# A two-layer diffusion backbone: the second FFN's down projections interleaved with seven-product up steps, and four smaller edits

## The chip, the cores and the metric

One core of one Trainium2 chip. The metric is the device time of one execution in microseconds (us), the median of several runs. The kernel computes in fp32 accuracy: each matrix product is made of three matmuls of operands that were split in a high and a low part.

## The reference

A batch of one, 512 tokens of width 1024, with 256 context tokens. Layer 0 mixes by attention (four global and four windowed heads, rotary positions, a sink), layer 1 by a Fourier transform over tokens and over channel groups, followed by a linear map. Each layer ends with a gated FFN with a width-3 convolution over tokens; every part is normed before and after, and modulated by vectors that come from the condition c.

```python
def conv_ffn(h, w_up, conv_w, conv_b, w_down):
    u = h @ w_up
    up = jnp.pad(u, ((0, 0), (1, 1), (0, 0)))
    u = up[:, :-2] * conv_w[0] + up[:, 1:-1] * conv_w[1] + up[:, 2:] * conv_w[2] + conv_b
    gate, val = jnp.split(u, 2, axis=-1)
    return (jax.nn.silu(gate) * val) @ w_down
...
        if i % 2 == 0:
            y, yc = attention_mixers(h, hc, ...)
        else:
            y = fourier_mix(h) @ w_f
        x = x + g1 * rms_norm(y, norm_g[i, 1])
        h = modulate(rms_norm(x, norm_g[i, 2]), sh2, sc2)
        x = x + g2 * rms_norm(conv_ffn(h, ffn_w_up[i], ...), norm_g[i, 3])
```

The FFN's inner width is 2816, which is 22 chunks of 128.

## The kernel before, in words

Tokens lie along the free dimension: `xT`, `yT`, `hh` and `hl` hold 8 chunks of 128 channels by 512 tokens. `hh` and `hl` are the high and low part of the normed input. `mm3` (lines 97 to 100) makes one product as three matmuls: high by high (L98), low by high (L99) and high by low (L100). `split` (L120, listed as L121) makes the two parts: a cast on ScalarE gives the high part (`wh`, `xh`), a subtraction on VectorE the low part (`wl`, `xl`). In a product the first two matmuls need only the cast of the weights; the third needs the subtraction as well. Weights are loaded by SyncE's queue into three rotating `raw` places and split into five rotating pairs `wh`, `wl`.

An FFN runs 22 up steps, one for each chunk `fi` of the inner width, in three groups `GROUPS` of 8, 6 and 8 chunks. A plain step makes gate and value with 48 matmuls of 512 columns. A seven-product step (`seven_products`, L1138, for the steps in `SEVEN`) computes the same from seven products of half the size in the manner of Strassen, with 84 matmuls of 256 columns; its weights need sums first (`raw` from `raw`, L1124 to L1127), then four splits, here called A (product 1), B (5 and 7), C (6 and 3) and D (2 and 4). ScalarE copies halves of the two results (L1160, L1163), and VectorE adds them (L1166, L1169). After a step the convolution is one ScalarE operation (L1220) and two VectorE taps (L1221, L1223) for each of gate and value, then SiLU, the product of both (L1234), and its split.

After the steps of a group, its down projections follow: for each of the 8 output chunks `d`, one load and split of `w_down`, 3 matmuls of 512 columns for each inner chunk of the group, and a copy (first group) or an add on VectorE (L1341) into `yT`. In the second FFN `pump` advances a modulation product (gemv) between those of group 0: a weight tile `mod_r` is multiplied by a scalar column and added into `gacc` on VectorE (L422, L425).

The order of instructions on each engine is laid out when the program is built, by the order in which the code asks for them and by what each waits for; `follow` adds an order between two instructions. Each engine then takes its instructions in that order.

Other places that the change touches: the attention's projections in groups kb, vb, qa (L841 on), with a gemv (`gemv_early`) pumped between; the first statistic at the start (Squares of `xT` on ScalarE, L652, and a table load, L604); the Fourier weights (`fourier_weights`, L1485 on); the last update of `xT` and the output (L1576 to L1581).

## Time and profile before

| | us |
|---|---|
| median of 3 runs | 1147.99 (1147.73 to 1148.07) |
| the profiled execution | 1147.63 |
| its span | 1145.9 |
| TensorE busy | 1115.4 |
| VectorE busy | 872.4 |
| ScalarE busy | 577.6 |
| GpSimd busy | 176.6 |

The granted TensorE clock of the profiled execution was 0.993. A row of the profile names engine (PE is TensorE, PEld its weight loads, DVE VectorE, ACT ScalarE, POOL GpSimd, SP SyncE), line, operation, and the tiles written and read. In groups the columns are the count, the busy time and the mean in nanoseconds, then idle time ahead of the group and what ended it. Rows of a timeline begin with the start and the duration in us; an operation may start before the one ahead of it has drained, so the pace of a row of operations is read from start to start.

### The profile page before, as it was taken

What the parts mean: (1) busy time and instruction counts of PE and PEld (TensorE: products, weight loads), DVE (VectorE), ACT (ScalarE), POOL (GpSimd) and SP (SyncE); (2) the same over time, 40 slices, a digit from 0 to 9 for tenths busy, and PEclk for the clock granted to TensorE, in tenths of its full rate; (3) what the DMA queues carried; (4) which work ended last, traced back from release to release, by engine and by line L of the source; (5) the groups of instructions that cost most, each with busy time, mean ns of one, the idle gap of its engine ahead of it and who ended that gap; (6) DMA issues with size and microseconds to landing.
All of it is one profiled execution on the core that took longest, in us unless ns stands there. A gap on an engine that the chain in (4) does not pass through costs nothing.

```text
span 1145.9 us, 19121 instructions
## 1 busy us (share of the span) xinstructions
PE 1115.4 (97%) x7658; PEld 962.8 (84%) x7658; DVE 872.4 (76%) x1418; ACT 577.6 (50%) x1030; POOL 176.6 (15%) x184
## 2 busy tenths in 40 slices
PE   8999999999999999999999999899999999999995
PEld 5689988868898978887898898879887888899895
DVE  4678777765679976987998668878997498679745
ACT  4342356666665633552465445557743355256442
POOL 1136332521420000000000143610000000000023
PEclk9999999999999999999999999999999999999998
DMA  9676101075142355535525301920227123223212
GB/s 366 248 239 215 43 1 38 8 263 208 38 184 111 117 194 207 218 122 209 187 108 183 122 2 37 291 88 28 74 95 270 58 92 111 101 84 111 93 56 74
DMA packets 31745, 151.61 MB, mean 132 GB/s; under 512 B 3236, under 2 KB 7972, under 8 KB 19752
## 3 DMA queue, kind: packets, MB, share of 16 engines
q1 hardware_dynamic: 30504, 146.19, 35.9%
q0 software_dynamic: 1152, 4.19, 1.5%
q8 instruction: 60, 0.98, 0.4%
q14 instruction: 29, 0.24, 0.1%
HBM read 146.18 MB, written 4.19 MB: 131 GB/s over the span
## 4 chain that ended last, share of the span: by engine, by line
PE 84%; DVE 7%; ACT 5%; DMA 2%; issue 1%; POOL 0%; DVEq 0%; SPq 0%; ACTq 0%; POOLq 0%
PE mm L98 24%; PE mm L99 23%; PE mm L100 23%; PE PT L920 1%; ACT wh L121 1%; PE O L98 1%; PE gm L498 1%; PE gm L98 1%; PE O L99 1%; PE gm L100 1%; PE gm L99 1%; PE mm L173 1%; PE O L100 1%; DVE md_t L230 1%; DMA xT<-in_mod_r 1%
## 5 line engine op out<-in xcount | busy, mean ns | idle before, releaser
L121 ACT CAST wh<-raw 128x1024 fp32r<-128x1024 f32 (+2 forms) x189 | 180.4, 966 | 188.8 <-PE mm L99 131.3
L121 DVE TENSOR_TENSOR wl<-raw,wh 128x1024 fp32r<-128x1024 f32 (+3 forms) x179 | 203.4, 1144 | 62.8 <-ACT wh L121 62.5
L98 PE MATMUL mm<-hh,wh 128*128 128x256 f32 (+2 forms) x652 | 220.8, 339 | 1.4 <-ACT yT L895 1.0
L99 PE MATMUL mm<-hl,wh 128*128 128x256 f32 (+2 forms) x652 | 218.4, 335 | 0.0
L100 PE MATMUL mm<-hh,wl 128*128 128x256 f32 (+2 forms) x652 | 218.1, 335 | 0.0
L272 POOL TENSOR_TENSOR gacc<-gacc,sq 128x256 f32<-128x256 f32 (+1 forms) x33 | 28.4, 862 | 714.2 <-ACT sq L270 713.5
L98 PEld LDWEIGHTS mm<-hh,wh 128*128 128x128 f32 x652 | 122.5, 188 | 18.9 <-ACT sq L1160 2.8
L99 PEld LDWEIGHTS mm<-hl,wh 128*128 128x128 f32 x652 | 122.6, 188 | 14.0
L100 PEld LDWEIGHTS mm<-hh,wl 128*128 128x128 f32 x652 | 122.6, 188 | 13.8
L98 PE MATMUL mm<-xh,wh 128*128 128x512 f32 (+1 forms) x368 | 132.0, 359 | 0.0
L99 PE MATMUL mm<-xl,wh 128*128 128x512 f32 (+1 forms) x368 | 130.8, 356 | 0.0
L100 PE MATMUL mm<-xh,wl 128*128 128x512 f32 (+1 forms) x368 | 130.3, 355 | 0.0
L98 PE MATMUL mm<-zh,wh 128*128 128x256 f32 x304 | 86.8, 286 | 0.0
L99 PE MATMUL mm<-zl,wh 128*128 128x256 f32 x304 | 84.6, 278 | 0.0
L100 PE MATMUL mm<-zh,wl 128*128 128x256 f32 x304 | 84.3, 277 | 0.0
L98 PEld LDWEIGHTS mm<-xh,wh 128*128 128x128 f32 x368 | 69.3, 188 | 12.8 <-issue 2.1
L99 PEld LDWEIGHTS mm<-xl,wh 128*128 128x128 f32 x368 | 69.2, 188 | 11.1 <-issue 0.4
L100 PEld LDWEIGHTS mm<-xh,wl 128*128 128x128 f32 x368 | 69.2, 188 | 10.8
L1220 ACT ACTIVATE cv<-mm,cols 128x512 f32<-128x512 f32 x64 | 49.6, 776 | 26.5 <-PE mm L100 23.5
L98 PEld LDWEIGHTS mm<-zh,wh 128*128 128x128 f32 x304 | 57.2, 188 | 3.5 <-ACT sq L1163 2.7
L100 PEld LDWEIGHTS mm<-zh,wl 128*128 128x128 f32 x304 | 57.2, 188 | 0.0
L99 PEld LDWEIGHTS mm<-zl,wh 128*128 128x128 f32 x304 | 57.1, 188 | 0.0
(423 smaller groups left out, 2669.3 us busy)
## 6 DMA issues: line engine op xcount, KB each, us to landing
raw<-in_w_up SPq DMA_DIRECT2D x42, 1024.0 KB, 4.9
xT<-in_mod_r SPq DMA_DIRECT2D x20, 1024.0 KB, 4.9
raw<-in_w_down SPq DMA_DIRECT2D x32, 512.0 KB, 4.2
raw<-in_mod_p SPq DMA_DIRECT2D x8, 1024.0 KB, 5.0
raw<-in_w_in SPq DMA_DIRECT2D x6, 1024.0 KB, 7.9
raw<-in_w_down SPq DMA_DIRECT2D x16, 384.0 KB, 3.1
yT<-in_mod_r SPq DMA_DIRECT2D x10, 512.0 KB, 5.9
raw<-in_w_out SPq DMA_DIRECT2D x4, 1024.0 KB, 4.9
```

The source lines that it names most:

```text
L98: i = PE.matmul(out, lhsT=ah, rhs=bh, start=start, stop=False, skip_group_check=skip)
L99: PE.matmul(out, lhsT=ah, rhs=bl, start=False, stop=False, skip_group_check=skip)
L100: return i, PE.matmul(out, lhsT=al, rhs=bh, start=False, stop=stop, skip_group_check=skip)
L121: i = S.copy(out=h, in_=src), eng.tensor_tensor(out=l, in0=src, in1=f(h), op=ALU.subtract)
L173: PE.matmul(ps[:32, :src.shape[1]], lhsT=ones32, rhs=src, start=True, stop=True)
L230: V.scalar_tensor_tensor(out=t, in0=src, scalar=am, in1=R, op0=ALU.mult, op1=ALU.mult)
L272: G.tensor_tensor(out=self.acc[:, sl], in0=self.acc[:, sl], in1=sq[:, sl], op=ALU.add)
L498: PE.matmul(ps[32 * q:32 * q + 32, :], lhsT=spad[:, k, :], rhs=w[:, q * T:(q + 1) * T], start=k == 0, stop=k == KC - 1)
L920: PE.transpose(out=pt[:, j * P:(j + 1) * P], in_=Ps[j][:, off:off + P], identity=ident)
L1220: S.activation(out=cv, in_=ps, func=AF.Identity, bias=bc, scale=wc[1])
```

## The change

The second FFN gets groups of its own: (0,4), (4,6), (10,6) and (16,6), each first chunk and length. All steps from 8 to 21 are seven-product steps. The down projections of the first three groups no longer stand in a block after their group: `DOWN` says how many of them are issued after each up step (four after steps 8 and 9, then one or two). The second gemv goes with the downs of group 1, one `pump` of two operations after each. `xT` is stored to DRAM while the FFN runs, its place takes some of the gate products, and it is loaded again for the end group. In the attention the order of projections is kb, qa, vb, the scores of the first queries are put into the last, and the gemv's second job has two places. A table for the reciprocal root is loaded at the end group of each FFN by an operation on `once`, and the start has a `follow` between Square and table load. Two Fourier weights are loaded early into `yT`. The last update of `xT` is one VectorE operation of 2 x 256 where VectorE and GpSimd did 256 each.

```diff
@@ -30,3 +30,3 @@
 
-GROUPS = [(0, 8), (8, 6), (14, 8)]
+GROUPS = [[(0, 8), (8, 6), (14, 8)], [(0, 4), (4, 6), (10, 6), (16, 6)]]
 
@@ -36,3 +36,5 @@
 
-SEVEN = [(5, 6, 8, 10, 12, 14, 15, 17, 18, 20), (8, 9, 11, 12, 14, 15, 17, 18, 20)]
+SEVEN = [(5, 6, 8, 10, 12, 14, 15, 17, 18, 20), (8, 9, 10, 11, 12, 13, 14, 15, 16, 17, 18, 19, 20, 21)]
+DOWN = {8: 4, 9: 4, 10: 1, 11: 1, 12: 1, 13: 2, 14: 1, 15: 2, 16: 1, 17: 1, 18: 1, 19: 2, 20: 1, 21: 2}
 NSKEW = [6, 5]
...
@@ -462,3 +465,3 @@
                 (l, v), k = jobs[n // KC], n % KC
-                ws[n] = places[n % len(places)]()
+                ws[n] = places[n % len(places) if n < KC else 3 + n % 2]()
                 SY.dma_start(out=ws[n], in_=a["mod_r"][6 * l + v - 2, k // 2][:, k % 2, :])
@@ -479,3 +482,6 @@
                                        op1=ALU.add)
-            load(n + len(places))
+            if n + len(places) < KC:
+                load(n + len(places))
+            for m in {3: (8,), 4: (9,)}.get(n, (n + 2,) if n >= KC else ()):
+                load(m)
             yield
@@ -603,3 +609,3 @@
             S.activation(out=scol, in_=cols[:, C_C:C_C + 16].rearrange("p (a b) -> p a b", a=2), func=AF.Silu)
-            S.activation(out=nsink, in_=scol[:, 0, 0:4], func=AF.Abs_reciprocal_sqrt)
+            ahead = S.activation(out=nsink, in_=scol[:, 0, 0:4], func=AF.Abs_reciprocal_sqrt)
             V.memset(maskb, 0.0)
@@ -651,3 +657,5 @@
                     else:
-                        S.activation(out=sq[:, :n], in_=src[:, k, :], func=AF.Square)
+                        i = S.activation(out=sq[:, :n], in_=src[:, k, :], func=AF.Square)
+                        if nsq[0] == 1:
+                            follow(i, ahead)
                     stat_add(ps, sq, n, k == 0, k == KC - 1)
...
@@ -840,3 +847,3 @@
             blocks = [(hh, hl, 0, 2), (hh, hl, 2, 4), (ch, cl, 0, 0)]
-            for g, kind in enumerate(["kb", "vb", "qa"]):
+            for g, kind in ((0, "kb"), (2, "qa"), (1, "vb")):
                 ws = group_weights(g)
...
@@ -851,3 +858,3 @@
                         pump(pr, 4)
-                        pump(gate, 2 if kind == "vb" else 1)
+                        pump(gate, 2 if kind == "qa" else 1)
                     if kind == "vb":
@@ -857,7 +864,6 @@
                     else:
-                        if t0 == 0:
-                            keys(0, [(mk(pps, [P, T], F32, "misc", 2), n) for n in (2, 4)])
-                        else:
-                            v_kv.append(values(0))
                         q_out(0, t0, ps)
+                    if kind == "vb" and kb == 2:
+                        keys(0, [(mk(pps, [P, T], F32, "misc", 2), n) for n in (2, 4)])
+                        v_kv.append(values(0))
 
...
@@ -1235,3 +1242,3 @@
             if (fi - f0) % 2 == 0:
-                gs["t"] = xp.pair([P, 2, T])
+                gs["t"] = places.pop(0) if l and (f0 == 0 or f0 == 10 and fi < 14) else xp.pair([P, 2, T])
             gh, gl = (t[:, (fi - f0) % 2, :] for t in gs["t"])
@@ -1240,2 +1247,26 @@
 
+        def down_part(gi, w, g_, d, hs, ps=None, end=False):
+            ps, sl = y_mm(pps, w, g_, hs, True, ps)
+            if gi == 0:
+                S.copy(out=yT[:, d, sl], in_=ps[:, sl])
+            else:
+                V.tensor_tensor(out=yT[:, d, sl], in0=yT[:, d, sl], in1=ps[:, sl], op=ALU.add)
+            if end:
+                ys.add(pps, yT[:, d, sl], hs)
+        def down_weights(gi, nch, d, pairs):
+            r = raw([P, nch, P], a["w_down%d%d" % (l, gi)][d])
+            wh, wl = pairs([P, nch, P])
+            split(wh, wl, r)
+            return [(wh[:, c, :], wl[:, c, :]) for c in range(nch)]
+        def down_tiles(gi, nch, g_):
+            yield
+            for d in range(KC):
+                down_part(gi, down_weights(gi, nch, d, wpair), g_, d, [0, 1])
+                if gi:
+                    pump(gem, GP[1])
+                yield
 
@@ -1297,2 +1328,5 @@
             remod(1, *n2, R[1], eng=V)
+            SY.dma_start(out=away, in_=xT)
+            xp2 = mk(cp, [P, 2, 2, 2, T], F32R, "xT")
+            places = [(xp2[:, i, 0], xp2[:, i, 1]) for i in (0, 1, 0, 1)]
             first[skew] = first[skew][:3] + (mk(pps, [P, T], F32, "mm", 6),)
@@ -1316,4 +1350,5 @@
             :, :, NF:], scalar1=-1.0, scalar2=None, op0=ALU.mult)
-        for gi, (f0, nch) in enumerate(GROUPS):
-            end = gi == len(GROUPS) - 1
+        down = iter(())
+        for gi, (f0, nch) in enumerate(GROUPS[l]):
+            end = gi == len(GROUPS[l]) - 1
             for fi in range(max(f0, FIRST), f0 + nch):
@@ -1332,3 +1367,13 @@
                     pump(gem, GP[0])
+                if l:
+                    pump(down, DOWN.get(fi, 0))
+            pump(down, 100)
+            if l and end:
+                xT = mk(cp, [P, KC, T], F32, "xT")
+                SY.dma_start(out=xT, in_=away)
             g_ = [gs[fi] for fi in range(f0, f0 + nch)]
+            if l and not end:
+                down = down_tiles(gi, nch, g_)
+                pump(down)
+                continue
             ws = {}
@@ -1336,15 +1381,6 @@
             def part(d, hs, ps=None):
-                ps, sl = y_mm(pps, ws[d], g_, hs, True, ps)
-                if gi == 0:
-                    S.copy(out=yT[:, d, sl], in_=ps[:, sl])
-                else:
-                    V.tensor_tensor(out=yT[:, d, sl], in0=yT[:, d, sl], in1=ps[:, sl], op=ALU.add)
-                if end:
-                    ys.add(pps, yT[:, d, sl], hs)
+                down_part(gi, ws[d], g_, d, hs, ps, end)
 
             def weights(d):
-                r = raw([P, nch, P], a["w_down%d" % gi][l, d])
-                wh, wl = (xp.spare if end and 4 <= d < 7 else wpair)([P, nch, P])
-                split(wh, wl, r)
-                ws[d] = [(wh[:, c, :], wl[:, c, :]) for c in range(nch)]
+                ws[d] = down_weights(gi, nch, d, xp.spare if end and 4 <= d < 7 else wpair)
 
@@ -1354,2 +1390,4 @@
             if end:
+                S.activation(out=once, in_=g_[-1][0][:, 0:1].bitcast(F32), func=AF.Abs_reciprocal_sqrt, bias=eps, scale=0.0)
                 pump(gem, 100)
@@ -1484,4 +1522,10 @@
 
+        def fourier_load(d):
+            r = yT[:, 2 * d + 2:2 * d + 4, :].rearrange("p a (g i c) -> p (a g) i c", i=2, c=P)
+            SY.dma_start(out=r, in_=a["w_f"][d])
+            return r
         def fourier_weights(d, eng=G):
-            r = raw([P, 4, 2, P], a["w_f"][d])
+            r = f_first[d] if d < 2 else raw([P, 4, 2, P], a["w_f"][d])
 
@@ -1517,2 +1561,3 @@
         over_channels(2, 1)
+        f_first = [fourier_load(d) for d in range(2)]
         r1 = plain.columns(1, pps)
@@ -1578,4 +1623,3 @@
             V.tensor_tensor(out=t, in0=yT[:, k:k + 2, hb], in1=R.unsqueeze(1).to_broadcast([P, 2, HT]), op=ALU.mult)
-            for i, eng in enumerate((V, G)):
-                eng.tensor_tensor(out=xT[:, k + i, hb], in0=xT[:, k + i, hb], in1=t[:, i, :], op=ALU.add)
+            V.tensor_tensor(out=xT[:, k:k + 2, hb], in0=xT[:, k:k + 2, hb], in1=t, op=ALU.add)
             SY.dma_start(out=a["out"][:, k:k + 2, hb], in_=xT[:, k:k + 2, hb])
...
```

What this does to the order on VectorE. First, two neighbouring seven-product steps. In before this is step 18, second of a pair, whose weight tiles are raw_10783 and raw_10785; the names mm_10620 and cv_15xx belong to step 16's plain work and to step 17 (mm_10677).

```order
1258 L1223 SCALAR_TENSOR_TENSOR cv_1530_10645<-mm_10620,cols_64,cv_1530_10645 128x511
1259 L1127 TENSOR_TENSOR raw_10785<-raw_10785,raw_10783 128x512
1260 L1234 TENSOR_TENSOR cv_1530_10645<-cv_1526_10612,cv_1530_10645 128x512
1261 L121 TENSOR_TENSOR wl_10790<-raw_10783,wh_10789 128x512
1262 L121 TENSOR_TENSOR wl_10794<-raw_10785,wh_10793 128x1024
1263 L121 TENSOR_TENSOR xl_10652<-cv_1530_10645,xh_10651 128x512
1264 L121 TENSOR_TENSOR wl_10798<-raw_10785,wh_10797 128x1024
1265 L1166 TENSOR_TENSOR mm_10677<-mm_10677,sq_10679 128x512
1266 L121 TENSOR_TENSOR wl_10802<-raw_10783,wh_10801 128x1024
1267 L1169 TENSOR_TENSOR mm_10678<-mm_10678,sq_10680 128x512
1268 L1221 SCALAR_TENSOR_TENSOR cv_1547_10771<-mm_10677,cols_64,cv_1547_10771 128x511
1269 L121 TENSOR_TENSOR wl_10916<-raw_10913,wh_10915 128x1024
```

Now step 16 to step 17: mm_10612 and mm_10613 are the results of step 16, mm_10726 is its down, raw_10746 and raw_10748 and the wl tiles 10753, 10757, 10761 and 10765 are splits A to D of step 17.

```order
1268 L1172 TENSOR_TENSOR mm_10612<-mm_10612,sq_10614 128x512
1269 L1132 TENSOR_TENSOR raw_10748<-raw_10748,raw_10746 128x512
1270 L123 TENSOR_TENSOR wl_10753<-raw_10746,wh_10752 128x512
1271 L1228 SCALAR_TENSOR_TENSOR cv_1541_10706<-mm_10612,cols_64,cv_1541_10706 128x511
1272 L1175 TENSOR_TENSOR mm_10613<-mm_10613,sq_10615 128x512
1273 L1230 SCALAR_TENSOR_TENSOR cv_1541_10706<-mm_10612,cols_64,cv_1541_10706 128x511
1274 L1133 TENSOR_TENSOR raw_10748<-raw_10748,raw_10746 128x512
1275 L1228 SCALAR_TENSOR_TENSOR cv_1542_10710<-mm_10613,ncw_8780,cv_1542_10710 128x511
1276 L1253 TENSOR_TENSOR yT_68<-yT_68,mm_10726 128x512
1277 L1230 SCALAR_TENSOR_TENSOR cv_1542_10710<-mm_10613,ncw_8780,cv_1542_10710 128x511
1278 L123 TENSOR_TENSOR wl_10757<-raw_10748,wh_10756 128x1024
1279 L1241 TENSOR_TENSOR cv_1542_10710<-cv_1541_10706,cv_1542_10710 128x512
```

```order
1280 L123 TENSOR_TENSOR wl_10761<-raw_10748,wh_10760 128x1024
1281 L123 TENSOR_TENSOR xl_10717<-cv_1542_10710,xh_10716 128x512
1282 L123 TENSOR_TENSOR wl_10765<-raw_10746,wh_10764 128x1024
1283 L123 TENSOR_TENSOR wl_10877<-raw_10874,wh_10876 128x768
1284 L1130 TENSOR_TENSOR raw_10902<-raw_10900 128x1024
```

Before, the four splits stood ahead of the two PSUM adds and the taps of the step before, with one PSUM add between; now the taps and the add of the down (L1253) of the step before stand ahead of splits B, C and D.

Second, VectorE around the gemv (`gacc`). In before it stands among the downs of group 0, whose splits are wl of 128x1024.

```order
1104 L422 TENSOR_SCALAR gacc_9229<-raw_9230,scol_77 128x1024
1105 L425 SCALAR_TENSOR_TENSOR gacc_9229<-raw_9230,scol_77,gacc_9229 128x1024
1106 L1221 SCALAR_TENSOR_TENSOR cv_1328_9161<-mm_9136,cols_64,cv_1328_9161 128x511
1107 L1223 SCALAR_TENSOR_TENSOR cv_1328_9161<-mm_9136,cols_64,cv_1328_9161 128x511
1108 L425 SCALAR_TENSOR_TENSOR gacc_9229<-raw_9238,scol_77,gacc_9229 128x1024
1109 L1234 TENSOR_TENSOR cv_1328_9161<-cv_1324_9128,cv_1328_9161 128x512
1110 L425 SCALAR_TENSOR_TENSOR gacc_9229<-raw_9238,scol_77,gacc_9229 128x1024
1111 L121 TENSOR_TENSOR xl_9074<-cv_1328_9161,xh_9073 128x512
1112 L121 TENSOR_TENSOR wl_9245<-raw_9242,wh_9244 128x1024
1113 L425 SCALAR_TENSOR_TENSOR gacc_9229<-raw_9274,scol_77,gacc_9229 128x1024 x2
1114 L121 TENSOR_TENSOR wl_9281<-raw_9278,wh_9280 128x1024
```

Now it stands among seven-product steps: here step 11 (mm_9765, mm_9766, with its down mm_9877) and the weights of step 12 (raw_9901, raw_9903, split A is wl_9908).

```order
1171 L428 SCALAR_TENSOR_TENSOR gacc_9738<-raw_9897,scol_78,gacc_9738 128x1024
1172 L1172 TENSOR_TENSOR mm_9765<-mm_9765,sq_9767 128x512
1173 L428 SCALAR_TENSOR_TENSOR gacc_9738<-raw_9897,scol_78,gacc_9738 128x1024
1174 L1175 TENSOR_TENSOR mm_9766<-mm_9766,sq_9768 128x512
1175 L1228 SCALAR_TENSOR_TENSOR cv_1426_9859<-mm_9765,cols_64,cv_1426_9859 128x511
1176 L1130 TENSOR_TENSOR raw_9903<-raw_9901 128x1024
1177 L1230 SCALAR_TENSOR_TENSOR cv_1426_9859<-mm_9765,cols_64,cv_1426_9859 128x511
1178 L1228 SCALAR_TENSOR_TENSOR cv_1427_9863<-mm_9766,ncw_8780,cv_1427_9863 128x511
1179 L1253 TENSOR_TENSOR yT_68<-yT_68,mm_9877 128x512
1180 L1230 SCALAR_TENSOR_TENSOR cv_1427_9863<-mm_9766,ncw_8780,cv_1427_9863 128x511
1181 L1132 TENSOR_TENSOR raw_9903<-raw_9903,raw_9901 128x512
1182 L1241 TENSOR_TENSOR cv_1427_9863<-cv_1426_9859,cv_1427_9863 128x512
```

```order
1183 L1133 TENSOR_TENSOR raw_9903<-raw_9903,raw_9901 128x512
1184 L123 TENSOR_TENSOR wl_9908<-raw_9901,wh_9907 128x512
1185 L123 TENSOR_TENSOR xT_8669<-cv_1427_9863,xT_8669 128x512
1186 L123 TENSOR_TENSOR wl_9912<-raw_9903,wh_9911 128x1024
1187 L123 TENSOR_TENSOR wl_9916<-raw_9903,wh_9915 128x1024
1188 L123 TENSOR_TENSOR wl_9920<-raw_9901,wh_9919 128x1024
```

The gemv moved from a stretch of downs alone into one where the sums of the next step's weights and its splits stand behind it.

Third, ScalarE at the start of the program: the Squares of `xT` and the two table loads, before and now.

```order
1 L603 ACT_TABLE_LOAD
2 L603 ACTIVATE scol_77<-cols_64 128x16
3 L652 ACTIVATE sqx_159<-xT_67 128x256
4 L604 ACT_TABLE_LOAD
5 L604 ACTIVATE nsink_86<-scol_77 128x4
6 L652 ACTIVATE sqx_159<-xT_67 128x256 x3
```

```order
1 L609 ACT_TABLE_LOAD
2 L609 ACTIVATE scol_78<-cols_64 128x16
3 L658 ACTIVATE sqx_160<-xT_67 128x256
4 L610 ACT_TABLE_LOAD
5 L610 ACTIVATE nsink_87<-scol_78 128x4
6 L658 ACTIVATE sqx_160<-xT_67 128x256 x3
```

One Square stands ahead of the second table load in both.

More of the change, by code (lines that the diff above doesn't have):

```diff
@@ L147 @@
     eps = mk(cp, [P, 1], F32, "eps")
+    once = mk(cp, [P, 1], F32, "once")
     V.memset(eps, EPS)
@@ L1646, in _layout @@
     out = {}
-    for h, (f0, n) in enumerate(GROUPS):
-        out["w_down%d" % h] = wd[:, f0:f0 + n].transpose(0, 3, 2, 1, 4)
+    for l, groups in enumerate(GROUPS):
+        for g, (f0, n) in enumerate(groups):
+            out["w_down%d%d" % (l, g)] = wd[l, f0:f0 + n].transpose(2, 1, 0, 3)
     wf = i["fourier_w_out"][0].reshape(4, 256, D)
```

4 lines of the change are left out of this document (2 added, 2 removed).

## The prediction

> **What bounds the kernel now.** I read the page first, then the waits of TensorE, then a table of stretches of the second FFN, then the groups of instructions there. The page's span, its TensorE row and its chain that ended last:
>
> ```profile
> span 1145.9 us, 19121 instructions
> PE 1115.4 (97%) x7658; PEld 962.8 (84%) x7658; DVE 872.4 (76%) x1418; ACT 577.6 (50%) x1030; POOL 176.6 (15%) x184
> PE 84%; DVE 7%; ACT 5%; DMA 2%; issue 1%; POOL 0%; DVEq 0%; SPq 0%; ACTq 0%; POOLq 0%
> ```
>
> TensorE sets the time: the change gains where it takes matmuls away, and loses wherever TensorE has to wait for something new. VectorE comes next. The profiled execution took 1147.63 us, 1.73 more than its span and 0.36 below the median of 1147.99; I sum against 1147.63 and add the 0.36 at the end. Differences under 0.2% (2.3 us) are what a measurement of this kernel can hardly tell from none.
>
> Next the stretches of the second FFN from up step 8 on, cut at the starts of matmuls. Columns: length, then busy time of each engine.
>
> ```profile
> core 0: us, PE busy (x) PEld busy (x) DVE busy (x) ACT busy (x) POOL busy (x), PEclk, DMA share, GB/s
> 903.46:924.22 20.76, 20.69 (x170) 19.98 (x169) 13.24 (x16) 12.26 (x20) 0.00 (x0) 1.00 0.31 109
> 924.22:935.42 11.20, 11.20 (x51) 9.01 (x50) 10.97 (x16) 6.43 (x10) 0.00 (x0) 1.00 0.04 16
> 967.26:1000.85 33.59, 33.59 (x145) 27.07 (x144) 20.39 (x25) 8.30 (x10) 0.00 (x0) 1.00 0.24 78
> 1064.58:1074.74 10.16, 10.16 (x85) 9.96 (x84) 6.55 (x9) 6.21 (x9) 0.00 (x0) 1.00 0.41 137
> sum 182.48, PE 182.22 PEld 161.77 DVE 140.17 ACT 94.53 POOL 0.00; mean PE 16.57 PEld 14.71 DVE 12.74 ACT 8.59 POOL 0.00
> ```
>
> Row 1 is two seven-product steps (8 and 9), row 2 a plain step (10), row 3 the eight down projections of group 1, row 4 a single seven-product step (20). The sum covers steps 8 to 21 and those eight downs, so the steps alone take 182.48 - 33.59 = 148.89 us. TensorE is never short of work here. The pace from start to start, from the timelines of TensorE and VectorE:
>
> ```profile
> 1063.88 0.39 PE L98 MATMUL mm<-hh,wh 128*128 128x512 f32 x1
> 1064.11 0.40 PE L99 MATMUL mm<-hl,wh 128*128 128x512 f32 x1
> 1064.58 0.28 PE L98 MATMUL mm<-hh,wh 128*128 128x256 f32 x1
> 1064.70 0.28 PE L99 MATMUL mm<-hl,wh 128*128 128x256 f32 x1
> 1010.02 1.23 DVE L121 TENSOR_TENSOR wl<-raw,wh 128x1024 fp32r<-128x1024 f32 x1 [5.31 <-ACT wh L121]
> 1011.16 0.69 DVE L1166 TENSOR_TENSOR mm<-mm,sq 128x512 f32<-128x512 f32 x1
> 1011.76 1.22 DVE L121 TENSOR_TENSOR wl<-raw,wh 128x1024 fp32r<-128x1024 f32 x1
> 1013.49 0.74 DVE L1221 SCALAR_TENSOR_TENSOR cv<-mm,cols,cv 128x511 f32<-128x511 f32 x1
> 1014.15 1.22 DVE L121 TENSOR_TENSOR wl<-raw,wh 128x1024 fp32r<-128x1024 f32 x1
> ```
>
> So a 512-column matmul costs 0.233 us (33.59/144), a 256-column one 0.12; on VectorE a split of 1024 costs 1.14, an operation of 512 costs 0.60, a conv tap 0.66.
>
> **The change, part by part.**
>
> *Five more seven-product steps.* Steps 10, 13, 16, 19 and 21 swap 48 matmuls of 512 columns for 84 of 256: 11.20 becomes 10.16, and all fourteen at 10.16 make 142.24 against 148.89: **-6.65 us**. (Without any wait inside a step, 84 x 0.118 = 9.9, and it would be -10.3; I keep the measured step.) The row weighs against a rule of the Trainium skill, "TensorE: Matmul & The Clock Gate", section "Back-to-back issue gap": it gives a sustained 131 ns per matmul at 512 columns and 81 ns at 128, which between them would be some 98 ns at 256, an estimate of mine; by that a seven-product step (8.2 us) would be slower than a plain one (6.3), and five of them would lose 9.7 us. The trace disagrees with both figures (0.233 and 0.12 us), so the sum goes by the rows.
>
> *The downs move into these steps.* Their matmul count is unchanged. The cover changes: in before, the 33.59 us of pure downs and the plain steps let VectorE run ahead, and its 5.31 us of idle time at 1010.02 is that lead. Now fourteen seven-product steps follow each other with one to four downs each. Rows of VectorE's groups in the second FFN, the last that of the modulation product (gemv), which stood among the downs of group 0 and now goes with those of group 1:
>
> ```profile
> L121 DVE TENSOR_TENSOR wl<-raw,wh 128x768 fp32r<-128x768 f32 x8 | 7.6, 953 | 3.2 <-ACT wh L121 3.2
> L1341 DVE TENSOR_TENSOR yT<-yT,mm 128x512 f32<-128x512 f32 x8 | 5.5, 685 | 11.2 <-PE mm L100 11.2
> L425 DVE SCALAR_TENSOR_TENSOR gacc<-raw,scol,gacc 128x1024 f32<-128x1024 f32 x7 | 9.0, 1283 | 1.8 <-DMA raw<-in_mod_r 1.7
> ```
>
> A seven-product step issues on VectorE the sums (1.14 + 0.60 + 0.60), splits A to D (0.60 + 3 x 1.14), two PSUM adds (1.20), four taps (2.64), the gate (0.60) and its split (0.60): 11.4 us. One down adds its weight split (0.953, some 0.87 by pace) and the yT add (0.60), together 12.9; TensorE takes 10.16 + 18 x 0.233 = 14.4. On average VectorE has time. In steps 10 to 13 two gemv operations (1.283 in the row, 1.2 by pace) per down make it 15.3, over TensorE's 14.4.
>
> The order decides. The rows above for step 16 to 17 put the taps of 16 and the yT add, which waits for TensorE's end of down 16, ahead of splits B, C and D of 17; VectorE's queue passes nothing. The L1341 row shows such an add idle for 1.4 us each time until the down is done. I replay it by hand, with the changed kernel's line numbers as in that order (L1130 to L1133 the sums, L1172 and L1175 the PSUM adds). Let 0 be the end of step 16's last product. The x sum L1172 is ready at -1.42 (12 x 0.118). Then on VectorE, ends: L1172 -0.8, L1132 -0.2, split A 0.4, tap 1.0, L1175 1.6, tap 2.3, L1133 2.9, tap 3.5, the add waits for the down (16 x 0.233 = 3.73) and ends 4.5, tap 5.2, **split B 6.3**, gate 6.9, **split C 8.0**, its split 8.6, **split D 9.8**. TensorE ends the down at 3.73, product 1 at 5.15, six matmuls that need only casts at 6.1, waits 0.3 for B, does ten until 7.6, waits 0.5 for C, does ten until 9.5, waits 0.4 for D, and has 46 left: 15.3. Without the waits it is 18 x 0.233 + 84 x 0.118 = 14.1. **1.2 us lost**, the same at 17 to 18, 18 to 19 and 20 to 21.
>
> The same for 11 to 12, where the gemv stands in front and even the sums and split A come after the taps: A ends at 7.9, TensorE has done its four early matmuls by 4.2 and waits 3.8, and 0.5 more for B: **4.3 lost**. For 12 to 13: 2.8. For 13 to 14 a second down covers: 1.6. For 14 to 15, 0.4; into 15, 16 and 20, which two downs cover, nothing; around 8 to 10 some 1.5 (1 at step 8, where the preload that the plain step 7 gave is gone). Sum 4.8 + 8.7 + 0.4 + 1.5 = **+15.4**. Bounds: each place could cost nothing if an engine's lead carries over, and the gemv loads could be later than I let them. They share three raw places with w_up, sums and w_down, and the page has for them:
>
> ```profile
> raw<-in_w_up SPq DMA_DIRECT2D x42, 1024.0 KB, 4.9
> yT<-in_mod_r SPq DMA_DIRECT2D x10, 512.0 KB, 5.9
> ```
>
> A load of 4.9 us that can start only when split D frees its place adds up to 2 us at each of three steps: +3 to +21, taken at 15.4. The place xT gives up:
>
> ```profile
> 778.97 0.41 DVE L299 TENSOR_TENSOR xT<-xT,md_t 128x256 f32<-128x256 f32 x1
> 810.54 0.61 ACT L121 CAST xh<-cv 128x512 fp32r<-128x512 f32 x1
> ```
>
> Its store can start with xT's last update and has 31 us until the first cast that will go there; in the end group the reload goes past w_down loads in SP's queue with downs of 4.2 us each ahead of it: 0, or 1 us if a weight comes late. Eight more yT adds are in the step sums.
>
> *Attention.* TensorE's waits, of which the second goes when queries stand ahead of values:
>
> ```profile
> PE mm L98 <- ACT wh L121: 2.3, 1, 2.3
> PE PT L949 <- DVE yT L771: 1.6, 1, 1.6
> PE misc L213 <- DVE Rs L210: 1.8, 2, 1.2
> ```
>
> -1.6 there. New: the second gemv job has only two places, each refilled in 5.9 us, and its end, which TensorE waits for, comes about 1.2 us after TensorE gets there. I take **-0.7** (-1.9 if loads are early, +1.5 if twice late).
>
> *Tables.* At the first FFN's end the load leaves the path of the statistic:
>
> ```profile
> 666.05 1.28 ACT L185 ACT_TABLE_LOAD   x1
> ```
>
> TensorE's 1.2 wait (L213) hangs on it and on a VectorE chain: **-0.6** (0 to -1.2). At the second FFN's end other halves cover TensorE: 0. At the start the order still has a Square ahead of the load, so this edit does not do what it says: 0, or +0.4 where a statistic comes later.
>
> *Fourier weights.* The 2.3 wait above, followed back in the chain:
>
> ```profile
> 719.40 6.71 DMA xh<-in_w_up
> 726.12 1.06 ACT xl L1091
> 728.97 0.95 ACT wh L121
> ```
>
> ScalarE is held by a slow xh load; the wh cast that TensorE waits for queues behind. Two weight loads fewer at that time quicken it; the order of ScalarE is unchanged: **-1.0** (0 to -2.3).
>
> *Tail.* VectorE and GpSimd add halves at once:
>
> ```profile
> 1136.55 1.29 DVE L1578 TENSOR_TENSOR sq<-yT,Rs 128x512 f32<-128x512 f32 x2
> 1137.76 1.81 DVE L1580 TENSOR_TENSOR xT<-xT,sq 128x256 f32<-128x256 f32 x2
> 1140.69 1.80 DVE L1580 TENSOR_TENSOR xT<-xT,sq 128x256 f32<-128x256 f32 x2
> ```
>
> Two L1580 take 1.8, 0.9 each; one operation of 512 should take the 0.6 of the L1578 rows: four times -0.3, with the last pair on the path of the store: **-0.7** (-1.2 to 0).
>
> Sum: -6.65 + 15.4 - 0.7 - 0.6 - 1.0 - 0.7 = **+5.75**; 1147.63 + 5.75 + 0.36 = **1153.7 us**.
>
> **The rivals.**
>
> *VectorE keeps up (faster).* The order is only a list; if VectorE's lead at steps 8, 9, 13, 15 (TensorE 18.5 with two downs of six chunks, 21.3 with four of four; VectorE 14 to 17) survives through five wh and wl places, the stalls shrink to 3. For it: the averages. Against: the places hold one step. 1153.7 - 12.4 = 1141.3. Chance 0.34. The sign turns where the stalls are 15.4 - 5.75 = 9.65.
>
> *Throughput alone (no change).* Steps 10 to 12 lose only VectorE's excess of 0.9 each, the others what I replayed: 2.7 + 4.8 + 1.9 = 9.4, so 1147.7. Chance 0.15.
>
> *The raw places (slower still).* Three gemv steps wait 2 us more for their loads: 1159.7. Chance 0.11. Decides where a w_up load starts behind a gemv load. Also for it: the 1.7 that L425 already waits for loads.
>
> My forecast has 0.40.
>
> The Trainium skill, "TensorE: Matmul & The Clock Gate", section "Architectural detail", calls VectorE's queue strictly first in, first out; a queue that let splits pass would be the first rival. No row here shows one passing.
>
> **How the numbers follow.** Faster by over 0.2% is the first rival: 0.34. Same: 0.15. Slower: 0.40 + 0.11 = 0.51. The range must reach both signs. The first rival spreads from 1135 (no stalls, the other edits at their best) to 1145.6; of its 0.34 I leave out 0.12 below 1139.5. Above, the third case with its spread up to 1160.5 leaves out 0.06. The forecast's own range is 1150.5 to 1157.
>
> **What would show it.** In the profile after: TensorE idle of 12 to 18 us between steps 8 and 21, released by the weight splits wl, most in steps 12 and 13; VectorE over 85% busy there; the tail shorter by 0.7; L949's wait gone. I am wrong if TensorE's idle time there is under 8 us, or if the waits are released by loads or by ScalarE's casts instead.

## The result, and the profile after

| | us |
|---|---|
| before, median of 4 runs | 1148.03 (1147.73 to 1148.86) |
| changed, median of 4 runs | 1165.11 (1161.86 to 1167.83) |
| ratio | 1.0144 (95% interval 1.0129 to 1.0160) |
| the profiled execution of the changed kernel | 1161.86, span 1160.1 |

The change costs 17.1 us; the forecast was 1153.7 with a range up to 1160.5, so the sign was right and the size a third. The changed kernel also scatters as the kernel before doesn't, and the profiled execution is its fastest: 14.2 us of span over before's. Its page:

```profile
span 1160.1 us, 19512 instructions
PE 1116.9 (96%) x7796; PEld 968.8 (84%) x7796; DVE 901.8 (78%) x1469; ACT 594.3 (51%) x1070; POOL 168.2 (14%) x180
PE 80%; DVE 11%; ACT 4%; DMA 3%; issue 2%; POOL 1%; DVEq 0%; SPq 0%; ACTq 0%; POOLq 0%
```

TensorE is busy as long as before, and of the chain 80% is TensorE's where it was 84%; VectorE has 11% for 7, the DMAs 3% for 2. So most of the time went into waits. Those of TensorE, over the whole span (what waited, for what; sum, count, longest):

```profile
PE mm L102 <- DVE wl L123: 8.2, 4, 3.3
PE misc L555 <- DVE mods L454: 5.3, 1, 5.3
PE mm L100 <- ACT wh L123: 2.8, 5, 1.9
```

Three of the first row's four waits, 7.2 us, are the stall that the prediction replayed, third matmuls that wait for a weight split; the fourth stands in the Fourier layer. The second row stands in the attention, where a small gain was forecast. By stages of the two traces: the attention's last scores start 3.1 us later, the second FFN starts 2.8 us later and takes 354.4 for 342.2 (from the last row spread of a norm ahead of it to the last norm's sum), and the tail behind TensorE's end takes 10.6 for 11.5.

From step 8 to the end of step 21, with the length first, then the busy time of TensorE, of its weight loads and of VectorE:

```profile
861.00:1104.25 243.25, 232.15 (x1536) 208.56 (x1535) 195.33 (x253) 125.66 (x198) 0.00 (x0) 0.99 0.32 112
```

TensorE is idle there for 11.1 us, just short of the 12 to 18 that the prediction named as its sign, with most of it in steps 12 and 13 and released by weight splits, as it said. VectorE is busy for 80%, not over 85%.

What the waits look like from VectorE, in the timeline of the changed kernel from step 11's taps to step 13's sums (start, duration, then in brackets idle time and its cause):

```profile
933.80 0.68 DVE L1253 TENSOR_TENSOR yT<-yT,mm 128x512 f32<-128x512 f32 x1
936.86 0.68 DVE L123 TENSOR_TENSOR wl<-raw,wh 128x512 fp32r<-128x512 f32 x1
938.06 4.36 DVE L123 TENSOR_TENSOR wl<-raw,wh 128x1024 fp32r<-128x1024 f32 x4
945.23 2.61 DVE L428 SCALAR_TENSOR_TENSOR gacc<-raw,scol,gacc 128x1024 f32<-128x1024 f32 x2 [2.81 <-DMA raw<-in_mod_r]
948.94 1.23 DVE L1130 TENSOR_TENSOR raw<-raw 128x1024 f32<-128x1024 f32 x1 [0.31 <-DMA raw<-in_w_up]
```

Split A of step 12 comes at 936.86, behind taps and the down's add, as the order says. Then the wait that the forecast kept as a rival: the gemv stands idle for 2.81 us for its tile, and step 13's sums behind it. The loads themselves, from the timeline of SyncE's queue:

```profile
940.44 0.33 SPq L132 DMA_DIRECT2D raw<-in_mod_r  x1
941.58 0.33 SPq L132 DMA_DIRECT2D raw<-in_w_up  x1
```

They start while the late splits run and free their places. Late splits make late loads, and since VectorE takes its operations in order, a wait for a late load holds back the sums and splits behind it.

A third thing shows in the table of stretches, whose column behind the engines is the granted clock of TensorE. The stretches are cut where that clock changes:

```profile
core 0: us, PE busy (x) PEld busy (x) DVE busy (x) ACT busy (x) POOL busy (x), PEclk, DMA share, GB/s
937.39:940.80 3.41, 3.20 (x15) 3.20 (x16) 3.41 (x5) 2.68 (x4) 0.00 (x0) 0.50 0.00 0
940.80:946.00 5.20, 5.14 (x41) 4.74 (x41) 2.39 (x3) 0.74 (x2) 0.00 (x0) 1.00 0.84 317
957.87:961.28 3.41, 3.41 (x16) 3.31 (x16) 3.41 (x4) 1.43 (x4) 0.00 (x0) 0.50 0.14 31
```

TensorE's waits of 3.3 and 2.8 us end at 937.60 and 956.64. The clock falls 0.2 us ahead of the first end and 1.2 us behind the second, stands at half for 3.4 us each time and is then at 1.00 again. At full clock TensorE's work in rows 1 and 3 would have taken 3.20 x 0.5 = 1.6 and 3.41 x 0.5 = 1.7 us less. Not all of this is new: ahead of the tail, the profiled execution of the kernel before has two such stretches and that of the changed kernel three, so of the 14.2 us the clock accounts for some 1.7.

### The profile page after: what moved, and what is told of

Read it like the earlier page. It is cut to its first block, busy times and chain, and to the rows that moved or that the text cites. A ratio compares the mean times of both kernels' runs of the same rounds, so it can differ in the third digit from the quotient of the medians.

```text
span 1160.1 us, 19512 instructions
## 1 busy us (share of the span) xinstructions
PE 1116.9 (96%) x7796; PEld 968.8 (84%) x7796; DVE 901.8 (78%) x1469; ACT 594.3 (51%) x1070; POOL 168.2 (14%) x180
## 4 chain that ended last, share of the span: by engine, by line
PE 80%; DVE 11%; ACT 4%; DMA 3%; issue 2%; POOL 1%; DVEq 0%; SPq 0%; ACTq 0%; POOLq 0%
PE mm L100 23%; PE mm L102 21%; PE mm L101 21%; DVE wl L123 2%; PE PT L926 1%; DMA cT<-in_mod_r 1%; PE gm L100 1%; PE gm L102 1%; PE gm L101 1%; PE O L100 1%; DMA raw<-in_w_up 1%; PE gm L504 1%; ACT wh L123 1%; PE O L101 1%; DVE md_t L233 1%
## 5 line engine op out<-in xcount | busy, mean ns | idle before, releaser
L123 DVE TENSOR_TENSOR wl<-raw,wh 128x1024 fp32r<-128x1024 f32 (+2 forms) x197 | 214.0, 1102 | 49.4 <-ACT wh L123 49.0
L102 PE MATMUL mm<-hh,wl 128*128 128x256 f32 (+1 forms) x632 | 204.4, 324 | 7.2 <-DVE wl L123 7.2
L100 PE MATMUL mm<-hh,wh 128*128 128x256 f32 (+1 forms) x632 | 207.3, 328 | 2.2 <-ACT yT L901 1.0
L101 PE MATMUL mm<-hl,wh 128*128 128x256 f32 (+1 forms) x632 | 203.8, 323 | 0.0
L100 PE MATMUL mm<-zh,wh 128*128 128x256 f32 x384 | 109.9, 286 | 2.0 <-ACT sq L1164 1.3
L100 PE MATMUL mm<-xh,wh 128*128 128x512 f32 (+1 forms) x302 | 107.5, 356 | 0.0
L102 PE MATMUL mm<-zh,wl 128*128 128x256 f32 x384 | 107.5, 281 | 0.0
L101 PE MATMUL mm<-zl,wh 128*128 128x256 f32 x384 | 107.4, 280 | 0.0
L101 PE MATMUL mm<-xl,wh 128*128 128x512 f32 (+1 forms) x302 | 107.1, 355 | 0.0
L102 PE MATMUL mm<-xh,wl 128*128 128x512 f32 (+1 forms) x302 | 106.2, 352 | 0.0
```

The costliest lines, as they stand in the source:

```text
L100: i = PE.matmul(out, lhsT=ah, rhs=bh, start=start, stop=False, skip_group_check=skip)
L101: PE.matmul(out, lhsT=ah, rhs=bl, start=False, stop=False, skip_group_check=skip)
L102: return i, PE.matmul(out, lhsT=al, rhs=bh, start=False, stop=stop, skip_group_check=skip)
L123: i = S.copy(out=h, in_=src), eng.tensor_tensor(out=l, in0=src, in1=f(h), op=ALU.subtract)
```

## The experiments

First the parts, each alone on the kernel before.

**ffn2_alone**: before, with only the second FFN's part of the change (`GROUPS`, `SEVEN`, `DOWN`, `down_tiles`, xT's place).

> The kernel before with only the second FFN's part of the change (groups, fourteen seven-product steps, interleaved downs, xT away). Both theories of the second FFN expect most of the loss here: 11 to 15 us over the kernel before, 1159 to 1163. If the attention carried the loss instead, it would be under 3 us.

1158.09 against 1147.02, ratio 1.0097 (1.0078 to 1.0115): 11.1 us slower, where my terms made 8.75.

**attention_alone**: before, with the order of projections and the gate's places.

> The kernel before with only the attention's new order and the two places of the gate's gemv. The trace of the changed kernel has a new wait of 5.3 us for the end of that gemv, and the wait of 1.6 at L949 is gone: 3 to 4 us slower, 1151 to 1152. My prediction's term was 0.7 faster, 1147.3.

1150.93, ratio 1.0034 (1.0021 to 1.0046): 3.9 slower. The old wait at L949 is gone, and TensorE has this one:

```profile
PE misc L552 <- DVE mods L451: 4.4, 1, 4.4
```

The chain of waits that leads to it holds a load:

```profile
100.80 7.09 DMA cT<-in_mod_r
```

It took 7.1 us into a place that had only just come free. But TensorE does not wait for this gemv's end. `mods` here is the addition, 0.15 us long, that finishes the gemv's first job; its input comes from two transposes (L452) of that job. In the changed kernel, where the load took 7.0 us and TensorE has stood still since 106.8:

```profile
100.58 0.38 PE L452 MATMUL misc<-con,yT 128*128 128x128 f32 x2
106.70 2.95 DVE L481 SCALAR_TENSOR_TENSOR sqx<-cT,scol,sqx 128x1024 f32<-128x1024 f32 x2 [1.78 <-DMA cT<-in_mod_r]
109.58 2.29 DVE L123 TENSOR_TENSOR wl<-raw,wh 128x1024 fp32r<-128x1024 f32 x1
111.79 0.15 DVE L454 TENSOR_TENSOR mods<-misc,cols 128x8 f32<-128x8 f32 x1
```

The input was complete at 101.0, and the addition ran at 111.79, since VectorE's order has the second job's operations, which wait for loads, and two weight splits ahead of it. It reads a `misc` tile, of which the kernel has two; the transposes of K (L555) write the next one and wait until it is free. So this wait, too, comes from VectorE's order. The clock follows here as well: in the changed kernel it stood at 0.50 for 3.4 us from 111.36 on.

**small_three**: before, with tables, Fourier weights and tail.

> The kernel before with only tables, Fourier weights and tail. My prediction's terms: 0.6 + 1.0 + 0.7 = 2.3 faster, about 1145. The difference of without_attention_part and ffn2_alone, measured on two chips, speaks for no gain or a loss of up to 2: 1147 to 1150.

1147.87 against 1147.01, ratio 1.0004 (0.9995 to 1.0013): nothing. TensorE's waits between the first FFN's end and the Fourier products were these in before, beside the two rows that the prediction shows (2.3 for wh, and of the row for Rs its longest, 1.2), a 0.8 for wl and a 0.3:

```profile
PE misc L98 <- DVE Z L121: 1.1, 2, 0.7
```

and in small_three:

```profile
PE misc L98 <- DVE Z L121: 2.2, 2, 1.5
PE mm L98 <- ACT wh L121: 1.8, 1, 1.8
```

The wait for Rs is gone, as forecast, with half a microsecond of that for wh and the 0.8 for wl; the wait for Z grew by 1.1. In all the waits fell from 5.7 to 4.0 us, yet no time was won. In this profiled execution the clock stood at half for 6.8 us behind the longer wait for Z, where that of the kernel before had 1.00 at the same place:

```profile
708.88:715.70 6.82, 6.79 (x31) 6.49 (x32) 2.92 (x9) 2.56 (x6) 0.00 (x0) 0.50 0.09 13
```

Whether the other executions have the same stretch is not known, so what ate the gain stays open.

**without_attention_part**: the whole change but the attention.

> The whole change but the attention's part. By the sum of parts measured (second FFN 1158.1, prediction's terms for tables, Fourier weights and tail together 2.3 faster): 1155 to 1158, against 1165.1 of the whole change.

1159.89, ratio 1.0110 (1.0095 to 1.0125), or 12.6 us slower, above the range I gave. It agrees with the parts, 11.1 + 0.9 = 12.0; with the attention's 3.9 they make 15.9 of the 17.1.

Then the second FFN's loss, with the second FFN's part alone as the base (1158.09); the diffs of this part are against it.

**gemv_without_loads**: the gemv's operations kept, its four loads left out.

```diff
                 if not places:
-                    load()
-                w = ws[n]
+                    w = hh[:, 0:4, :].rearrange("p (i a) c -> p i (a c)", i=2).bitcast(F32)
+                else:
+                    w = ws[n]
```

> The second FFN's part alone, with the gemv's VectorE operations kept in place but reading a tile that is there already, so that its four loads of 1 MB are left out (the modulation vector it makes is not the reference's). Theory 1, VectorE's order and time: 0 to 2 us less than the second FFN's part alone. Theory 2, the loads through three raw places hold VectorE (7.7 us of VectorE's waits for them and 2.9 for w_up behind them in the changed kernel's trace): 4 to 8 us less.

1144.50, ratio 0.9975 (0.9966 to 0.9985): 13.6 us less, more than either theory allowed, and faster than before. The stretches from down 10 to the end of step 13's products, and from down 16's bulk three steps on, in ffn2_alone:

```profile
910.70:963.09 52.39, 46.04 (x310) 41.87 (x309) 43.60 (x55) 23.89 (x39) 0.00 (x0) 0.97 0.38 141
1017.83:1064.63 46.80, 44.92 (x309) 40.48 (x308) 38.95 (x52) 24.14 (x39) 0.00 (x0) 1.00 0.29 100
```

and in gemv_without_loads:

```profile
913.03:956.45 43.42, 43.42 (x309) 40.06 (x307) 39.64 (x54) 25.58 (x40) 0.00 (x0) 1.00 0.32 110
1009.58:1053.01 43.43, 43.43 (x309) 40.07 (x307) 39.65 (x54) 25.49 (x40) 0.00 (x0) 1.00 0.33 110
```

Three steps and three downs take 43.4 us without a wait, with VectorE 91% busy: 9.0 us less in the first stretch, and 3.4 less in steps 17 to 19, where no gemv runs in either kernel. But this run does not keep the rest equal. With no loads to reckon with, the build puts splits B and C ahead of the taps, and it puts all eight of the gemv's operations ahead of the first stretch, the last four here:

```profile
883.02 2.60 DVE L428 SCALAR_TENSOR_TENSOR gacc<-hh,scol,gacc 128x1024 f32<-128x1024 f32 x2
886.14 2.60 DVE L428 SCALAR_TENSOR_TENSOR gacc<-hh,scol,gacc 128x1024 f32<-128x1024 f32 x2
```

So loads, the gemv's operations and the order were still mixed.

**splits_first** and **splits_before_taps** ask for the next step's weights ahead of this step's taps; the second also asks for each down's weights one down earlier (the last three lines).

```diff
+                    xy = seven_products(l, fi, pps, bs, early.pop(fi, None))
+                    if l and fi + 1 in SEVEN[l]:
+                        early[fi + 1] = seven_weights(l, fi + 1)
+                    cc = [conv(fi, i, u, None, i == 1) for i, u in enumerate(xy)]
...
+                down_part(gi, w, g_, d, [0, 1])
+                if d + 1 < KC:
+                    w = down_weights(gi, nch, d + 1, wpair)
```

> The second FFN's part alone, gemv and loads where the change has them, but the sums and splits of the next step are asked for before the taps of this step, so that VectorE's order has splits B, C and D mostly ahead of the taps again. Theory 1, the order: 1145 to 1150. Theory 2, loads that come late whatever the order is: 1155 to 1158.

> As splits_first, but the weights of each down are asked for one down earlier, so that their casts no longer stand behind the next step's on ScalarE, which is what TensorE waited for in splits_first. Theory 1, the order of splits and taps on VectorE sets the loss: 1145 to 1150. Theory 2, the gemv's loads hold VectorE whatever the order is: 1153 to 1158, with VectorE waiting for mod_r and w_up as in ffn2_alone.

1192.69 (ratio 1.0395, 1.0371 to 1.0419) and 1165.86 (1.0165, 1.0151 to 1.0179): both slower as a whole and outside what either theory gave, and by the whole I would have called theory 1 dead. The stretch that the theory speaks of says otherwise. Down 10 to step 13, with the gemv and its loads in place, in splits_before_taps:

```profile
924.26:967.74 43.48, 43.43 (x308) 40.13 (x307) 42.37 (x54) 23.25 (x37) 0.00 (x0) 1.00 0.46 166
```

And TensorE's waits over its up steps and downs:

```profile
PE mm L100 <- ACT wh L123: 9.5, 9, 3.9
PE mm L102 <- DVE wl L123: 3.6, 2, 1.8
```

43.48 us, with six of the gemv's operations inside as in ffn2_alone, and none of them waits for its tile:

```profile
948.10 2.60 DVE L427 SCALAR_TENSOR_TENSOR gacc<-raw,scol,gacc 128x1024 f32<-128x1024 f32 x2
```

The same loads cost nothing there once the splits stand ahead of the taps. So it is not the loads as such that cost the 9.0 us, and late loads come of the late order. There is a limit to this: VectorE enters the stretch with a lead, having waited 5.9 us for a cast just ahead of it, and is busy for 42.37 of the 43.48, so it is not shown that more such steps in a row would run free. What the kernel loses instead is around steps 8, 9 and 13, where several downs meet and their casts queue on ScalarE behind those of the next step. How much the gemv's loads add on top of a late order was not run by itself; with a late order and no gemv, steps 17 to 19 lose 3.4.

**gemv_with_group0**, **gemv_in_plain_steps**, **gemv_in_first_ffn**, **gemv_first_ffn_later** and **gemv_first_ffn_single** put the gemv elsewhere, for example

```diff
-                if gi:
-                    pump(gem, GP[1])
...
+                if l and fi < 8:
+                    pump(gem, GP[1])
```

and, in the last three, `gemv_jobs([(1, v) for v in range(6)], pps, away)` in the first FFN.

> The second FFN's part alone, but its gemv pumped with every other down of group 0 (steps 8 and 9, four downs each) where it went with group 1. If the gemv steps carry the loss, by VectorE's time or by late loads, 6 to 9 us of it go: 1151 to 1155, unless the same waits come at steps 8 and 9. If the order of splits behind taps carries it whatever stands between, under 3 us go.

> The second FFN's part alone, with its gemv pumped after the plain steps 3 to 7, where one w_up load is all that uses the raw places, and not at all between seven-product steps. If the gemv's loads among seven-product steps are the cause, as gemv_without_loads (1144.5) suggests, the same here with a full computation: 1144 to 1147. If what helped there was only the work of loading left out, no place is good, and it stays at 1153 to 1158.

> The second FFN's part alone, with its gemv done among the first FFN's five, whose loads have the stored-away place of xT, and none in the second FFN. If the gemv's loads through the raw places are the cause of the loss, the second FFN takes what it took without loads, less its gemv operations, and the first FFN hides 10 us of VectorE work: 1142 to 1146. If the first FFN can't hide it: 1148 to 1155.

> As gemv_in_first_ffn, but in the first FFN two pumps only after plain steps from 9 on, one before, as in the kernel before. gemv_in_first_ffn lost 4.2 us to waits near its steps 4 and 5, which its doubled pumps brought, and its second FFN was 3.5 us shorter than before's. If both readings hold, the 4.2 go and the whole is 2 to 4 us faster than the kernel before: 1143 to 1145. If the first FFN has no room for the job at any place: 1148 to 1152.

> As gemv_in_first_ffn, with one pump at each place; the sixth job then falls into the first FFN's end group, where 10 us of VectorE work meet the statistics and the reload of xT. If the end group hides it, 1143 to 1145; if the next part waits for the reload, up to 1150.

1155.70, 1153.90, 1151.56, 1151.87 and 1155.19, ratios 1.0074 (1.0059 to 1.0089), 1.0058 (1.0043 to 1.0073), 1.0043 (1.0027 to 1.0058), 1.0050 (1.0037 to 1.0062) and 1.0073 (1.0060 to 1.0087). All five missed what I hoped for. With group 0, VectorE waited 21.2 us for w_up, and kept doing so long after the gemv's last operation at 900.4: the order stays late, and the loop of late splits and late loads runs on with the w_up loads alone. In the plain steps TensorE waited twice for splits, 6.7 us, up to step 8, and the steps behind ran without a wait, with the splits early again. In the first FFN the second FFN shrank to 338.5 to 338.8 us, 3.4 to 3.7 under before's 342.2, while the first grew by 7.8 to 11.9. The last of them waits for the gemv itself:

```profile
PE misc L441 <- DVE gacc L427: 6.4, 1, 6.4
```

The kernel before had the gemv beside the eight-chunk downs of group 0, where VectorE was busy for 33.01 of 49.97 us. The change takes that place away, and none of these five is as good.

**attention_five_places** and **attention_earlier_pumps** ask what makes the attention's wait, with diffs against attention_alone. In the first the second job's tiles lie in `yT` where queries write meanwhile, so its modulation vector is not the reference's.

```diff
-                ws[n] = places[n % len(places) if n < KC else 3 + n % 2]()
+                ws[n] = places[n % len(places)]()
...
-                        pump(gate, 2 if kind == "qa" else 1)
+                        pump(gate, 2 if kind != "vb" else 1)
```

> The attention's new order alone, but the gemv's second job keeps the five places that it had. If the two places make the new wait of 4.4 us, that wait shrinks by over 3 us: 1146 to 1148. If the new order itself, by which TensorE needs that gemv's result no later but has less work ahead of it, makes it, or if the five places now wait for queries that use them: 1150 to 1152.

> The attention's part alone, with the gemv pumped two at a time in the block kb as well. The chain of the wait ends in a load of 7.1 us into one of two places, issued when the gemv's operation before frees it; six operations pumped earlier bring the chain forward: the wait of 4.4 shrinks by 2 to 4 us, 1147 to 1149. If the place, not the pump, sets when each load starts from the beginning of the second job on, nothing changes: 1151.

1150.29 (ratio 1.0019, 1.0009 to 1.0029) and 1155.39 (1.0080, 1.0066 to 1.0094). With five places 3.3 us of the wait remain: `mods` still stands behind the second job, which now waits 5.5 us for GpSimd's work on `yT`. With earlier pumps `mods` runs at 100.1 and the wait for it is gone, but there are two others, 3.3 for a weight split and 3.7 for the gemv's own end. No run asked for `mods` ahead of the second job and left the rest alone; that this would take the wait away is argued, not shown.

Last, an arrangement that keeps the gemv where it was. **downs_of_group1_only** interleaves only group 1's downs, and makes steps 16, 19 and 21 seven-product steps.

```diff
+GROUPS = [[(0, 8), (8, 6), (14, 8)], [(0, 8), (8, 6), (14, 8)]]
+SEVEN = [(5, 6, 8, 10, 12, 14, 15, 17, 18, 20), (8, 9, 11, 12, 14, 15, 16, 17, 18, 19, 20, 21)]
+DOWN = {n: 1 for n in range(14, 22)}
...
-            if l and not end:
+            if l and gi == 1:
                 down = down_tiles(gi, nch, g_)
```

> A third arrangement: the groups and the block of group 0's downs with the gemv stay as in the kernel before; only group 1's eight downs are interleaved, one after each of steps 14 to 21, and steps 16, 19 and 21 become seven-product steps. Nothing is added to the raw places there. If the loss came from the gemv meeting seven-product steps, the three steps keep their 1.0 us each: 2 to 4 us faster than the kernel before, 1143 to 1145. If interleaving itself loses (VectorE's order, 1.1 us a step as in steps 16 to 20 of the change): 5 us slower, 1152.

> The same with the change's tail (one VectorE operation of 2 x 256). My prediction's term for the tail was 0.7, and the span behind the last matmul is 0.9 shorter in the changed kernel's trace: 0.5 to 1 us below downs_of_group1_only. If the tail were hidden behind the output's store: no difference.

1152.34 and 1153.51 (ratios 1.0051, 1.0038 to 1.0065, and 1.0052, 1.0040 to 1.0065): slower, and the first at the very number that I had given for a loss by interleaving itself, but by chance, since TensorE ended 4.4 us earlier than in before. The timeline of downs_of_group1_only behind it:

```profile
1134.70 1.29 DVE L301 TENSOR_TENSOR xT<-xT,md_t 128x256 f32<-128x256 f32 x2 [5.99 <-DMA xT<-away]
```

I had given xT's place to chunks that the end group reads to the last, so the reload started behind the last matmul. **group1_xT_for_8_to_11** gives it to chunks 8 to 11:

```diff
+                gs["t"] = places.pop(0) if l and 8 <= fi < 12 else xp.pair([P, 2, T])
```

> As downs_of_group1_only, but xT's place holds the gate products of chunks 8 to 11, which group 1's downs read last at step 21, where that run gave it to chunks 14 to 17, which the end group reads until TensorE's end. That run's second FFN was 2.7 us shorter and TensorE's end 4.4 earlier than in the kernel before, but its tail was 20.5 us against 11.5, since xT's reload could start only behind the last matmul. With the reload early: 9 us less, 1143 to 1145, 2 to 4 faster than the kernel before. If interleaving itself were bad: still 1152.

> The same with the change's tail in one VectorE operation. Nothing waits for the reload now, so the tail can show: 0.5 to 1 us below group1_xT_for_8_to_11, or no difference if the output's store hides it.

1144.45 against 1147.64, ratio 0.9973 (0.9962 to 0.9985), and with the tail 1143.88, ratio 0.9967 (0.9955 to 0.9979): 3.2 and 3.8 us faster than before, and by the ratios some 20 faster than the change. The two differ by no more than their intervals; the tail's operations are shorter in the trace all the same. Steps 14 to 21 with seven of the eight downs in the first:

```profile
968.22:1079.88 111.66, 111.65 (x799) 103.60 (x798) 96.17 (x127) 64.72 (x100) 0.00 (x0) 1.00 0.32 109
```

TensorE never waits, with VectorE at 96.17 of 111.66.

## Why the prediction was too low

Of the 11.3 us that the forecast lacks, the parts measured alone give the attention 4.6, the three small edits 3.2 and the second FFN 2.3; the remaining 1.2 belong to no part.

*Five more seven-product steps, -6.65.* Right in kind: where nothing waits, a step takes 10.3 us besides its down (43.42 less 54 matmuls of 0.233, over three steps; 111.66 less 126, over eight). Only half was ever seen as time, 3.4 to 3.7 us of the second FFN without a gemv.

*Stalls, +15.4.* The replay had the places and their ranking right: waits of 3.34, 2.77 and 1.08 us for splits at 11 to 12, 12 to 13 and 13 to 14 where it had 3.8, 2.8 and 1.6, and 15.6 us a step for 15.3 in steps 17 to 19. Over the first two of these the whole was larger, 9.0 us (52.39 against 43.42) for 7.1. Of the 9.0, TensorE was idle for 6.35 (52.39 - 46.04) and busy for 2.6 longer (46.04 against 43.42). The replay had no term for the clock, which stood at half from 934.44 to 937.85: 1.7 of the 2.6. The other 0.9 stays open.

*"VectorE's order" as the cause.* Right as far as it was tested. splits_before_taps has the loads, the gemv and an early order, and loses nothing in these steps. The loads are no surcharge of their own there, as the rival with 0.11 had them: they come late where the splits do. gemv_without_loads has an early order too, so it does not show that leaving out the loads is enough.

*Attention, -0.7 (bounds -1.9 and +1.5): measured +3.9.* This step failed outright. I took the end of the second gemv job for what TensorE waits for, and let it come 1.2 us late with loads of 5.9. TensorE waits for `mods` of the first job instead, which was ready at 101.0 and stood behind the second job and two splits in VectorE's order until 111.79; the last load among them took 7.0. That made a wait of 5.3 us in the changed kernel and 4.4 in attention_alone. L949's gain of 1.6 was real.

*Tables, Fourier weights, tail, -2.3: measured +0.9, in noise.* The forecast counted each wait that goes as time won. The wait for Rs went, and a wait for Z grew behind it, with the clock at half for 6.8 us in the one traced execution; I had named what hides each edit but not what is late next. The tail is right as an item (10.6 for 11.5 us), too small to be measured alone.

*What gives the scatter.* The four runs of the changed kernel, ordered: 1161.86 us at a mean granted clock of 0.992, 1164.94 at 0.988, 1165.28 at 0.986, 1167.83 at 0.984. The slower ones have the lower clock, which fits more stretches at half clock; it was not traced, since only the fastest run has a profile. The forecast had no term for it, and the median stands 3.3 us over the profiled run.

## What to carry to other kernels

A block in which TensorE is fully busy and VectorE idle is where side work lives for nothing: before it is cut up and interleaved, list what runs beside it (here a gemv with 4 MB of loads) and find a new home for that first. When an order looks bad in a replay, mend the order first, and follow the buffers too: a late read frees a place late and the next load starts late. Ask of each small operation that another engine needs what stands ahead of it in its queue: here an addition of 0.15 us was ready 10.8 us before it ran. When a place is lent to something else, ask when its last reader lets go. Judge an experiment by the stretch that its theory speaks of, since its total can go the other way for another reason.

## What the runs showed of the hardware

A wait on TensorE can cost more than its own length. With the waits of 3.3 and 2.8 us in the changed kernel came 3.4 us each at a granted clock of 0.50, in which 256-column matmuls started 0.21 us apart (938.19 and 938.40) instead of 0.12 (943.46 and 943.58). The length of the wait alone does not decide it. In ffn2_alone the same wait of 2.77 us, up to 952.85, was followed by full clock, and in the kernel before a wait of 2.3 us, up to 729.96, by half:

```profile
952.85:956.30 3.45, 3.45 (x27) 3.27 (x28) 3.45 (x4) 2.67 (x5) 0.00 (x0) 1.00 0.00 0
730.87:734.28 3.41, 3.41 (x17) 3.32 (x16) 3.38 (x3) 1.72 (x3) 3.41 (x3) 0.50 1.07 211
```

The Trainium skill, "TensorE: Matmul & The Clock Gate", section "What's actually happening", tells of a gate that looks at windows of about 3.4 us and halves the clock after an idle one, with a phase that differs from run to run. The half clock and the 3.4 us agree with it, and a phase would explain why equal waits fare differently; but a wholly idle window was not needed here, since TensorE had been at work again for 1.2 us when the clock fell at 957.87. As a rough price, an estimate from the rows above: 1.7 us for each such stretch in which TensorE is busy throughout.
